# Eight wide matmuls in a row and eight narrow ones in a row, instead of the two in turn: the feature blocks of a hybrid decoder layer

## The chip, the cores and the metric

The kernel runs on one core of a Trainium2 chip. The metric is device time in microseconds (us), the median over three runs. Everything on the core runs as a program of five engines with a queue each: TensorE (PE in the rows; PEld is its weight load), VectorE (DVE), ScalarE (ACT), GpSimd (POOL) and SyncE (SP), which issues the DMAs.

## What is computed

One decoder layer on 256 tokens of 2048 features: an input projection, two mixers side by side (a gated linear recurrence and a sparse attention that keeps 64 of up to 256 keys), a gated merge, an output projection with a layer norm, and a gated ConvFFN with a second layer norm. Cut to what matters here:

```python
h = einsum('btd,de->bte', x, w_in)                  # 2048 -> 12368 features
xr, gr, q, k, v, qi, ki, wi, g_rnn, g_att = split(h)
y_rnn = rg_lru(causal_dwconv(xr)) * gelu(gr)
y_att = dsa_attention(rope(q), rope(k), v, rope(qi), rope(ki), wi, topk)
merged = sigmoid(g_rnn) * y_rnn + sigmoid(g_att) * y_att
x = layer_norm(ALPHA * x + merged @ w_out)
u = causal_dwconv(einsum('btd,df->btf', x, w_up))    # 2048 -> 11264
gate, up = split(u)
x = layer_norm(ALPHA * x + (silu(gate) * up) @ w_down)
```

All of it is in float32. The kernel makes each product from two halves of every operand: `hi`, the number rounded to the type that TensorE multiplies fast (float32r), and `lo`, what is left. A product is hi*hi + hi*lo + lo*hi.

## The kernel before

**Two kinds of product.** A *feature block* (`feature_block`, L161) makes 128 output features on the partitions with the 256 tokens as columns. The moving operand is `xt` (later `x1t`, the same buffer): for each of the 16 slices `k` of the 2048 input features, 512 columns, of which the first 256 are the tokens' hi and the others their lo. The stationary operand is a 128x128 piece of the weights. Per slice there are two matmuls into one PSUM bank of 512 columns: `high()` (L169, its matmul at L170) multiplies all 512 columns by the weight's hi, so that columns 0 to 255 collect hi*hi and 256 to 511 the cross term; `low()` (L173, L174) multiplies the 256 hi columns by the weight's lo and adds to columns 256 to 511. A block is 16 such pairs, high before low, but for the last slice, where the low comes first so that the high closes the bank. There are 181 feature blocks: 1 (80 features wide) and 8 of the indexer, 4 of the keys, 32 of the attention (`q`, `ga`), 48 of the recurrence (`xr`, `gr`, `gn`) and 88 of the ConvFFN (`gate`, `up`).

A *token tile* (`token_tile`, `token_half`, L190 to L202) has tokens on the partitions and 512 features as columns. Here the weights are the moving operand, and all its matmuls are 512 columns wide (L197, L199, L201). Values (`psv`), output projection (`pso`) and `w_down` (`psd`) are made so, and the change doesn't touch them.

**Weights.** A list `order` names the weight tiles (128 x 2048 float32, 1 MB) in the order of use. `load_to` (L102) issues their DMAs on SyncE's queue up to four tiles ahead, into three buffers `raw`. `split_half` (L112) makes hi with ScalarE (L116) and lo with VectorE (L119), for one half of a tile (eight slices) at a time; hi and lo have four buffers of half a tile each, so two tiles. `weights` (L136) asks for the split of the tile after the one that is used next. So a half of hi or lo comes free when the last matmul that reads it is done.

**Around a block.** `project` (L185) makes a block and hands it to a function that evacuates it (`evacuate`, L311: ScalarE copies columns 256 to 511, VectorE adds columns 0 to 255), then `tick` (L146) runs work that was put off by `after` for a number of blocks: the indexer's products (`pl`), the top-k on VectorE (L400, L401), the attention's scores (`ps_s`, L452 to L456, 256 columns each), transposes (`pt`) and gathers (`po`, L487 to L489, 512 columns each), and the recurrence's gates (`pg`, L555 to L557, six matmuls of 256 columns). These stand in TensorE's queue between two blocks. The order of each engine's queue comes from a scheduler that keeps to the program's dependencies and its priorities; it is fixed when the program is built.

Of the kernel before, what the change touches and what calls it, by code (L numbers as in the profile page):

```python
# [16 lines left out]
T = 256  # L17
D = 2048
KT = D // P
# [7 lines left out]
LRU_C = 8.0  # L27
# [7 lines left out]

# Column starts in w_in.
C_XR, C_GR, C_Q, C_K, C_V, C_QI, C_KI, C_GRNN, C_GATT = (
    0, 2048, 4096, 6144, 6656, 7168, 8192, 8272, 10320)

# Columns of the per-feature parameters.  # L40
O_CW, O_CB, O_BA, O_BI, O_LAM, O_G1, O_B1, O_FW, O_FB = (
    0, 64, 80, 96, 112, 128, 144, 160, 424)
N_PAR = 512
# Columns of the constants.
O_ID, O_CI, O_SI, O_PEN = 0, 128, 384, 640
# [4 lines left out]
def hybrid_layer(ctx, tc, x, xT, w_blk, w_ki, w_v, lru_w, par, w_o, w_u, w_d, lnrows, consts, rot, out):  # L50
    nc = tc.nc
# [5 lines left out]

    # ---------------------------------------------------------------- weights
    order = []
# [34 lines left out]
    done = {"load": 0, "split": 0}  # L94
# [42 lines left out]

    # Work that is to wait until some more weight tiles have gone through the tensor engine.
    later = []
# [19 lines left out]

    # Features on partitions, tokens free: columns 0..255 hi*hi, 256..511 the cross terms.  # L160
    def feature_block(key, src, m=P):  # L161
        halves = weights(key)
        ps = psum.tile([P, 512], F32, tag="b", name="psb", bufs=4)
        for k in range(KT):
            hi, lo = halves[k // 8]
            o = (k % 8) * m
            first, last = k == 0, k == KT - 1

            def high():  # L169
                nc.tensor.matmul(ps[:m, :], hi[:, o:o + m], src[:, k, :], start=first, stop=last,  # L170
                                 skip_group_check=True)

            def low():  # L173
                nc.tensor.matmul(ps[:m, T:], lo[:, o:o + m], src[:, k, :T], start=False, stop=False,  # L174
                                 skip_group_check=True)
            if last:
                low()
                high()
            else:
                high()  # L180
                low()
        return ps

    # A block, its evacuation and then whatever waited for it.
    def project(key, fn, src=None, m=P):  # L185
        fn(feature_block(key, xt if src is None else src, m))
        tick()

    # Tokens on partitions, 512 features free; src_hi/src_lo hold features on partitions.
    def token_half(halves, t, ps, k0, hi_at, lo_at, kn):  # L190
# [19 lines left out]

    # The last tiles of a product: the first 128 tokens go through all of them, then the others.
    def token_tiles_held(keys, pss, k0, src, pool, between):
# [13 lines left out]
    nsp = base.tile([P, KT], F32, name="nsp")  # L226
# [6 lines left out]

    # Layer norm of the 128 rows r, 512 columns after another; done(c) takes them.
    def norm(r, g, b, t, done):
# [28 lines left out]

    # ---------------------------------------------------------------- phase 1
    wide = pool("wide")
# [13 lines left out]
    for k0, k1 in zip(cuts, cuts[1:]):  # L280
        r = xraw[k0 // 8][:, k0 % 8 * T:(k0 % 8 + k1 - k0) * T]
        nc.sync.dma_start(r, xT[:, k0 * T:k1 * T])
        s = {0: 0, 4: 1}.get(k0)
        if s is not None:
            nc.sync.dma_start(ki_raw[:, s * kiw:(s + 1) * kiw], w_ki[:, s * kiw:(s + 1) * kiw])
        r = r.rearrange("p (k t) -> p k t", t=T)
        nc.scalar.copy(xt[:, k0:k1, :T], r)
        nc.vector.tensor_sub(xt[:, k0:k1, T:], r, xt[:, k0:k1, :T].bitcast(F32))
        if s is not None:
            splits[0].append(split_half(0, s, ki_raw, kiw))  # L290
    raw = new_raw("raw1")
    halves = [[wst.tile([P, 1024], F32R, tag=tag, name=f"{tag}1_{s}", bufs=4) for tag in ("hi", "lo")]
              for s in range(2)]
    for s in range(4):
        r = raw[:, s * 512:(s + 1) * 512]
        nc.sync.dma_start(r, order[1][1][:, s * 512:(s + 1) * 512])
        hi, lo = (h[:, s % 2 * 512:(s % 2 + 1) * 512] for h in halves[s // 2])
# [21 lines left out]

    # ---- indexer  # L320
    # Scores and attention weights keep queries 128..255 against all keys in columns 0..255,
    # queries 0..127 against keys 0..127 in columns 256..383.
    W2 = T + P
# [86 lines left out]

    # ---- keys and values
    # The parts of a key block lie side by side: keys 0..127 high, low, keys 128..255 high, low.
    kx = pa.tile([P, KV, 2, 2, P], F32R, name="kx")
# [23 lines left out]

    # ---- attention, one group of query heads after another
    def got_q(ps, n, g, pth, ptl):
# [66 lines left out]

    # ---- RG-LRU, four blocks of features at a time
    phm = ExitStack()
# [5 lines left out]

    # nsp = -LRU_C * softplus(-lambda), log1p by its series in e / (2 + e).
    lam = parm[:, O_LAM:O_LAM + KT]
    tiny = lambda name: work.tile([P, KT], F32, tag=name, name=name)
    e, z, z2, acc, neg = (tiny(s) for s in ("l_e", "l_z", "l_z2", "l_acc", "l_neg"))
# [45 lines left out]
    def recur(j0, v):  # L564
        xc, rg, ig, aa, th = (v[s] for s in ("xc", "rg", "ig", "aa", "th"))
        for i in range(NB):
            nc.scalar.activation(th[:, i], rg[:, i], AF.Tanh, scale=nsp[:, j0 + i:j0 + i + 1])
        for i in range(NB):
            nc.scalar.activation(aa[:, i], rg[:, i], AF.Exp, scale=nsp[:, j0 + i:j0 + i + 1])
        # 1 - a^2 = -tanh(log a) * (1 + a^2)  # L570
        nc.scalar.activation(rg, aa, AF.Square)
        nc.vector.scalar_tensor_tensor(th, rg, 1.0, th, op0=ALU.add, op1=ALU.mult)
        nc.scalar.activation(th, th, AF.Sqrt, scale=-1.0)
        nc.vector.tensor_mul(ig, ig, xc)
        nc.vector.tensor_mul(ig, ig, th)
        for i in range(NB):
            nc.vector.tensor_tensor_scan(rg[:, i], aa[:, i], ig[:, i], 0.0, op0=ALU.mult, op1=ALU.add)
# [30 lines left out]

    # ---------------------------------------------------------------- w_out and the first norm
    pho = ExitStack()  # L610
# [46 lines left out]

    # ---------------------------------------------------------------- ConvFFN
    phf = ExitStack()
# [27 lines left out]

    # ---------------------------------------------------------------- w_down and the second norm
    phd = ExitStack()
# [29 lines left out]
def _constants():  # L719
    def angles(rd):  # L720
        half = rd // 2
        inv = np.power(THETA, -np.arange(half, dtype=np.float64) * 2.0 / rd).astype(np.float32)
        ang = np.arange(T, dtype=np.float32)[:, None] * inv[None, :]
        return np.cos(ang.astype(np.float64)).T, np.sin(ang.astype(np.float64)).T

    c = np.zeros((P, N_CONST), np.float32)
    c[:, O_ID:O_ID + P] = np.eye(P)
    cos, sin = angles(16)
    c[:, O_CI:O_CI + T] = 1.0
    for r in (0, 64):  # L730
        c[r:r + 8, O_CI:O_CI + T] = cos
        c[r + 8:r + 16, O_CI:O_CI + T] = cos
        c[r:r + 8, O_SI:O_SI + T] = -sin
        c[r + 8:r + 16, O_SI:O_SI + T] = sin
    cos, sin = angles(32)
    rot = np.zeros((32, 2 * T), np.float32)
    rot[:16, :T], rot[16:, :T] = cos, cos
    rot[:16, T:], rot[16:, T:] = -sin, sin
    # Queries 128..255 against all keys, then queries 0..127 against keys 0..127.
    q = np.arange(P)[:, None]  # L740
    c[:, O_PEN:O_PEN + T] = np.where(np.arange(T)[None, :] > q + P, CAUSAL_FILL, 0.0)
    c[:, O_PEN + T:O_PEN + T + P] = np.where(np.arange(P)[None, :] > q, CAUSAL_FILL, 0.0)
    return c, rot
# [62 lines left out]
```

## Time and profile before

| | us |
|---|---|
| median of 3 runs | 1472.03 |
| lowest, highest | 1469.31, 1472.29 |
| profiled execution: span (nothing stands around it) | 1469.3 |
| TensorE busy | 1430.9 (97%) |
| VectorE busy | 1008.9 (69%) |
| ScalarE busy | 760.5 (52%) |
| GpSimd busy | 269.3 (18%) |

| stage | us from the span's start |
|---|---|
| first block (`ki`) | 5 to 15 |
| indexer and keys (13 blocks with the first) | 5 to 96 |
| values (token tiles) | 96 to 124 |
| attention (32 blocks) | 124 to 328 |
| recurrence (48 blocks) | 328 to 615 |
| output projection, first norm | 615 to 718 |
| ConvFFN (88 blocks) | 718 to 1218 |
| `w_down`, second norm | 1218 to 1469 |

How to read it: a matmul's recorded duration reaches over the start of the next one, since they are pipelined, so busy time of TensorE is no measure of its speed. What tells is the distance from one start to the next. In the timeline, rows that follow each other with the same text are merged (x2), and then the row has the first one's start.

### The profile page before, as it was taken

What the parts mean: (1) busy time and instruction counts of PE and PEld (TensorE: products, weight loads), DVE (VectorE), ACT (ScalarE), POOL (GpSimd) and SP (SyncE); (2) the same over time, 40 slices, a digit from 0 to 9 for tenths busy, and PEclk for the clock granted to TensorE, in tenths of its full rate; (3) what the DMA queues carried; (4) which work ended last, traced back from release to release, by engine and by line L of the source; (5) the groups of instructions that cost most, each with busy time, mean ns of one, the idle gap of its engine ahead of it and who ended that gap; (6) DMA issues with size and microseconds to landing.
All of it is one profiled execution on the core that took longest, in us unless ns stands there. A gap on an engine that the chain in (4) does not pass through costs nothing.

```text
span 1469.3 us, 19909 instructions
## 1 busy us (share of the span) xinstructions
PE 1430.9 (97%) x7718; PEld 1222.6 (83%) x7718; DVE 1008.9 (69%) x1462; ACT 760.5 (52%) x1068; POOL 269.3 (18%) x227
## 2 busy tenths in 40 slices
PE   7989999999999999999799999999999999999996
PEld 6868888888888888888688888888888888888885
DVE  5787766777777777665776777677767775545456
ACT  4444555568777777644344444444444444433342
POOL 3541122220020211110422112211221120000002
PEclk9999999999999999999899999999999999999998
DMA  7435544545545454576355555555555557555552
GB/s 270 161 135 192 180 142 168 186 164 194 203 155 215 143 201 152 192 300 215 143 190 183 183 190 190 183 182 191 189 185 182 191 188 272 206 207 198 190 199 86
DMA packets 42205, 275.41 MB, mean 187 GB/s; under 512 B 4576, under 2 KB 4832, under 8 KB 10240
## 3 DMA queue, kind: packets, MB, share of 16 engines
q1 hardware_dynamic: 42112, 274.16, 52.2%
q8 instruction: 60, 0.98, 0.3%
q14 instruction: 33, 0.27, 0.1%
HBM read 269.94 MB, written 4.19 MB: 187 GB/s over the span
## 4 chain that ended last, share of the span: by engine, by line
PE 91%; DVE 4%; POOL 2%; DMA 1%; issue 1%; ACT 0%; SPq 0%; ACTq 0%; POOLq 0%; DVEq 0%
PE psb L170 44%; PE psb L174 22%; PE psd L201 5%; PE psd L197 5%; PE psd L199 5%; PE pso L201 2%; PE pso L199 2%; PE pso L197 2%; DVE lo L119 1%; DMA cst<-in_consts 1%; POOL qf L333 0%; POOL sh L332 0%; DMA xraw<-in_xT 0%; DVE rg L247 0%; PE psv L199 0%
## 5 line engine op out<-in xcount | busy, mean ns | idle before, releaser
L170 PE MATMUL psb<-xt,hi 128*128 128x512 f32 (+1 forms) x2896 | 1022.7, 400 | 6.4 <-ACT hi L116 5.4
L119 DVE TENSOR_TENSOR lo<-raw,hi 128x1024 fp32r<-128x1024 f32 (+2 forms) x488 | 609.9, 1253 | 361.7 <-ACT hi L116 352.1
L174 PE MATMUL psb<-xt,lo 128*128 128x256 f32 (+1 forms) x2896 | 786.1, 282 | 1.5 <-DVE lo L119 1.3
L116 ACT CAST hi<-raw 128x1024 fp32r<-128x1024 f32 (+1 forms) x488 | 509.5, 1048 | 365.8 <-PE psd L201 126.9
L170 PEld LDWEIGHTS psb<-xt,hi 128*128 128x128 f32 (+1 forms) x2896 | 536.8, 188 | 125.2 <-ACT hi L116 5.4
L174 PEld LDWEIGHTS psb<-xt,lo 128*128 128x128 f32 (+1 forms) x2896 | 547.9, 189 | 18.8 <-DVE lo L119 3.5
L683 POOL TENSOR_TENSOR y<-y 128x256 f32<-128x256 f32 x44 | 68.1, 1549 | 383.8 <-DVE y L675 362.3
L197 PE MATMUL psd<-hi,fh 128*128 128x512 f32 x352 | 136.9, 389 | 0.0
L199 PE MATMUL psd<-lo,fh 128*128 128x512 f32 x352 | 136.9, 389 | 0.0
L201 PE MATMUL psd<-hi,fl 128*128 128x512 f32 x352 | 136.9, 389 | 0.0
L675 DVE SCALAR_TENSOR_TENSOR y<-u,parm,y 128x255 f32<-128x255 f32 (+1 forms) x176 | 85.1, 484 | 6.2
L199 PEld LDWEIGHTS psd<-lo,fh 128*128 128x128 f32 x352 | 66.1, 188 | 13.8
L201 PEld LDWEIGHTS psd<-hi,fl 128*128 128x128 f32 x352 | 66.1, 188 | 13.7
L197 PEld LDWEIGHTS psd<-hi,fh 128*128 128x128 f32 x352 | 66.1, 188 | 13.5
L313 ACT COPY ev<-psb 128x256 f32<-128x256 f32 (+1 forms) x181 | 65.6, 362 | 0.8 <-PE psb L170 0.8
L684 ACT CAST fh<-y 128x256 fp32r<-128x256 f32 x44 | 17.9, 407 | 90.8 <-POOL y L683 90.8
L238 POOL TENSOR_SCALAR rstd<-mv 128x1 f32<-128x1 f32 x4 | 3.1, 778 | 294.8 <-DVE mv L236 294.8
L199 PE MATMUL pso<-lo,mh 128*128 128x512 f32 x128 | 49.9, 390 | 0.0
L197 PE MATMUL pso<-hi,mh 128*128 128x512 f32 x128 | 49.9, 390 | 0.0
L201 PE MATMUL pso<-hi,ml 128*128 128x512 f32 x128 | 49.8, 389 | 0.0
L331 POOL TENSOR_TENSOR qf<-qf,rots 32x256 f32<-32x256 f32 x16 | 15.5, 971 | 151.6 <-DVE sh L330 151.6
L681 ACT ACTIVATE y<-y 128x256 f32<-128x256 f32 x44 | 18.4, 419 | 47.0 <-DVE y L675 47.0
(172 smaller groups left out, 1028.0 us busy)
## 6 DMA issues: line engine op xcount, KB each, us to landing
raw<-in_w_blk SPq DMA_DIRECT2D x91, 1024.0 KB, 4.8
raw<-in_w_u SPq DMA_DIRECT2D x88, 1024.0 KB, 4.7
raw<-in_w_d SPq DMA_DIRECT2D x44, 1024.0 KB, 4.7
raw<-in_w_o SPq DMA_DIRECT2D x16, 1024.0 KB, 4.8
raw<-in_w_v SPq DMA_DIRECT2D x4, 1024.0 KB, 4.8
lwr<-in_lru_w SPq DMA_DIRECT2D x4, 512.0 KB, 3.7
g<-in_lnrows SPq DMA_DIRECT2D x2, 1024.0 KB, 6.6
xres<-in_x SPq DMA_DIRECT2D x4, 512.0 KB, 7.3
```

The costliest lines, as they stand in the source:

```text
L116: nc.scalar.copy(hi[:, :w], raw[:, s * w:(s + 1) * w])
L119: eng.tensor_sub(lo[:, o:o + step], raw[:, s * w + o:s * w + o + step], hi[:, o:o + step].bitcast(F32))
L170: nc.tensor.matmul(ps[:m, :], hi[:, o:o + m], src[:, k, :], start=first, stop=last, skip_group_check=True)
L174: nc.tensor.matmul(ps[:m, T:], lo[:, o:o + m], src[:, k, :T], start=False, stop=False, skip_group_check=True)
L197: nc.tensor.matmul(ps, hi_at(k, t), hi[:, o:o + 512], start=first, stop=False, skip_group_check=True)
L199: nc.tensor.matmul(ps, hi_at(k, t), lo[:, o:o + 512], start=False, stop=False, skip_group_check=True)
L201: nc.tensor.matmul(ps, lo_at(k, t), hi[:, o:o + 512], start=False, stop=last, skip_group_check=True)
L313: nc.scalar.copy(t[:m], ps[:m, T:])
L675: nc.vector.scalar_tensor_tensor(y[:, s:], u[:, :T - s], w(tap), y[:, s:], op0=ALU.mult, op1=ALU.add)
L681: nc.scalar.activation(yg, yg, AF.Silu)
L683: nc.gpsimd.tensor_mul(yg, yg, yu)
L684: nc.scalar.copy(fh[:, j], yg)
```

## The change

The 32 matmuls of a feature block stay as they are, with the same operands, and come in another order: for the first half of the slices eight highs and then eight lows; for the second half seven highs, eight lows and the last high. The rest of the difference is in comments alone, so line numbers move: the high's matmul is L166 in the changed kernel, the low's L171.

```diff
     def feature_block(key, src, m=P):
         halves = weights(key)
         ps = psum.tile([P, 512], F32, tag="b", name="psb", bufs=4)
-        for k in range(KT):
-            hi, lo = halves[k // 8]
-            o = (k % 8) * m
-            first, last = k == 0, k == KT - 1
-
-            def high():
-                nc.tensor.matmul(ps[:m, :], hi[:, o:o + m], src[:, k, :], start=first, stop=last,
-                                 skip_group_check=True)
-
-            def low():
-                nc.tensor.matmul(ps[:m, T:], lo[:, o:o + m], src[:, k, :T], start=False, stop=False,
-                                 skip_group_check=True)
-            if last:
-                low()
-                high()
-            else:
-                high()
-                low()
+        def high(k):
+            hi, o = halves[k // 8][0], k % 8 * m
+            nc.tensor.matmul(ps[:m, :], hi[:, o:o + m], src[:, k, :], start=k == 0, stop=k == KT - 1,
+                             skip_group_check=True)
+
+        def low(k):
+            lo, o = halves[k // 8][1], k % 8 * m
+            nc.tensor.matmul(ps[:m, T:], lo[:, o:o + m], src[:, k, :T], start=False, stop=False,
+                             skip_group_check=True)
+
+
+        for s in range(2):
+            ks = range(8 * s, 8 * s + 8)
+            for k in ks[:8 - s]:
+                high(k)
+            for k in ks:
+                low(k)
+        high(KT - 1)
         return ps
```

On TensorE, the border of the last two ConvFFN blocks before (`hi_1` and `lo_1` are the second halves of a tile's weights, `hi_0` and `lo_0` the first of the next; 512 or 256 is the number of columns):

```order
L174 MATMUL psb<-xt,lo_1_11175 128x256
L170 MATMUL psb<-xt,hi_1_11174 128x512
L174 MATMUL psb<-xt,lo_1_11175 128x256 x2
L170 MATMUL psb<-xt,hi_1_11174 128x512
L170 MATMUL psb<-xt,hi_0_11224 128x512
L174 MATMUL psb<-xt,lo_0_11225 128x256
L170 MATMUL psb<-xt,hi_0_11224 128x512
```

The same two blocks in the changed kernel, down to the first token tile of `w_down`:

```order
L166 MATMUL psb<-xt,hi_0_11170 128x512 x8
L171 MATMUL psb<-xt,lo_0_11171 128x256 x8
L166 MATMUL psb<-xt,hi_1_11174 128x512 x7
L171 MATMUL psb<-xt,lo_1_11175 128x256 x8
L166 MATMUL psb<-xt,hi_1_11174 128x512
L166 MATMUL psb<-xt,hi_0_11224 128x512 x8
L171 MATMUL psb<-xt,lo_0_11225 128x256 x8
L166 MATMUL psb<-xt,hi_1_11228 128x512 x7
L171 MATMUL psb<-xt,lo_1_11229 128x256 x8
L166 MATMUL psb<-xt,hi_1_11228 128x512
L197 MATMUL psd<-hi_0_11276,fh 128x512
```

Each high left its low; the last high of a block and the first eight of the next are now nine in a row.

On VectorE, between the keys' last blocks and the value product (`score` is the top-k's table, `lo_0` a half of the first value tile's weights, `kx` the keys):

```order
 L389 SCALAR_TENSOR_TENSOR score<-rl,wi,score 128x128
 L400 MAX m_990<-score 128x8
-L400 MAX m_993<-score 128x8
-L401 MATCH_REPLACE score<-m_990,score 128x256
-L401 MATCH_REPLACE score<-m_993,score 128x128
 L119 TENSOR_TENSOR lo_0_997<-raw_788,hi_0_996 128x1024
 L421 TENSOR_TENSOR kx<-kf,kx 128x2x128
+L401 MATCH_REPLACE score<-m_990,score 128x256
+L400 MAX m_993<-score 128x8
 L400 MAX m_1050<-score 128x8
+L401 MATCH_REPLACE score<-m_993,score 128x128
```

The split of the value weights and the keys' lo moved ahead of three small operations of the top-k. ScalarE's queue has a few such neighbours that changed places; those of GpSimd and SyncE are the same as before.

## Rows read from the trace of the kernel before

**Rows 1.** The page: busy us (share) xinstructions; the chain by line

```profile
PE 1430.9 (97%) x7718; PEld 1222.6 (83%) x7718; DVE 1008.9 (69%) x1462; ACT 760.5 (52%) x1068; POOL 269.3 (18%) x227
...
PE psb L170 44%; PE psb L174 22%; PE psd L201 5%; PE psd L197 5%; PE psd L199 5%; PE pso L201 2%; PE pso L199 2%; PE pso L197 2%; DVE lo L119 1%; DMA cst<-in_consts 1%; POOL qf L333 0%; POOL sh L332 0%; DMA xraw<-in_xT 0%; DVE rg L247 0%; PE psv L199 0%
```

**Rows 2.** Stages: start:end, length, busy us (x) by engine, PEclk, DMA, GB/s

```profile
84.00:126.00 42.00, 38.14 (x178) 30.39 (x175) 35.72 (x88) 18.80 (x28) 11.10 (x12) 0.96 0.50 175
720.00:1218.00 498.00, 498.00 (x2814) 431.95 (x2814) 355.79 (x524) 240.12 (x350) 100.09 (x86) 1.00 0.52 183
```

**Rows 3.** Timeline of TensorE, ConvFFN: start us, us, engine line op tiles xcount

```profile
850.24 0.63 PE L170 MATMUL psb<-xt,hi 128*128 128x512 f32 x2
850.71 0.28 PE L174 MATMUL psb<-xt,lo 128*128 128x256 f32 x1
850.83 0.40 PE L170 MATMUL psb<-xt,hi 128*128 128x512 f32 x1
...
851.89 0.40 PE L170 MATMUL psb<-xt,hi 128*128 128x512 f32 x1
```

**Rows 4.** Timeline of TensorE, last feature block and first token tile

```profile
1217.71 0.40 PE L170 MATMUL psb<-xt,hi 128*128 128x512 f32 x1
1217.95 0.40 PE L197 MATMUL psd<-hi,fh 128*128 128x512 f32 x1
1218.18 0.39 PE L199 MATMUL psd<-lo,fh 128*128 128x512 f32 x1
...
1218.63 0.39 PE L197 MATMUL psd<-hi,fh 128*128 128x512 f32 x1
```

**Rows 5.** Timeline of TensorE, an LRU block right behind a gate product

```profile
508.96 0.40 PE L170 MATMUL psb<-xt,hi 128*128 128x512 f32 x1
...
514.29 0.62 PE L170 MATMUL psb<-xt,hi 128*128 128x512 f32 x2
```

**Rows 6.** Timeline of TensorE, deep in the token tiles of w_down

```profile
1300.23 0.39 PE L197 MATMUL psd<-hi,fh 128*128 128x512 f32 x1
```

**Rows 7.** Timeline of TensorE, gather product of attention

```profile
229.67 0.39 PE L487 MATMUL po<-pth,vh 128*128 128x512 f32 x1
...
231.76 0.39 PE L170 MATMUL psb<-xt,hi 128*128 128x512 f32 x1
```

**Rows 8.** Timeline of TensorE, an attention block and the scores behind it

```profile
199.01 0.39 PE L170 MATMUL psb<-xt,hi 128*128 128x512 f32 x1
...
204.66 0.28 PE L452 MATMUL ps_s<-kx,qh 128*128 128x256 f32 x1
...
205.25 0.49 PE L475 MATMUL pt<-ident,pr 128*128 128x128 f32 x3
```

**Rows 9.** Timeline of TensorE, LRU stage: start, a wait before gates, end

```profile
333.67 0.63 PE L170 MATMUL psb<-xt,hi 128*128 128x512 f32 x2
...
415.23 0.39 PE L170 MATMUL psb<-xt,hi 128*128 128x512 f32 x1
...
417.91 0.39 PE L170 MATMUL psb<-xt,hi 128*128 128x512 f32 x1
...
614.93 0.40 PE L197 MATMUL pso<-hi,mh 128*128 128x512 f32 x1
```

**Rows 10.** Waits of TensorE: us in total, times, longest

```profile
PE psv L199 <- DVE lo L119: 3.5, 3, 2.0
```

**Rows 11.** Timeline of TensorE, first block, with idle before and releaser

```profile
9.63 0.71 PE L170 MATMUL psb<-xt,hi 128*80 128x512 f32 x1 [0.98 <-DVE xt L288]
10.15 0.41 PE L174 MATMUL psb<-xt,lo 128*80 128x256 f32 x1
10.36 0.63 PE L170 MATMUL psb<-xt,hi 128*80 128x512 f32 x1
```

**Rows 12.** Timeline of TensorE, value product

```profile
112.06 0.40 PE L197 MATMUL psv<-hi,xt 128*128 128x512 f32 x1
...
114.36 0.39 PE L199 MATMUL psv<-lo,xt 128*128 128x512 f32 x1
```

## The prediction

> **What bounds the kernel now.** The page's busy table and chain come first: TensorE is busy nearly all the span, and two lines of the feature blocks, the 512-column matmul (below: a high) and the 256-column one (a low), hold 66% of the chain that ended last [rows 1]. So a nanosecond on the spacing of these matmuls counts, unless something else is late in that stage. The table by stage says where that is: in the ConvFFN stage (720 to 1218 us) TensorE is busy all 498 us, VectorE 356, ScalarE 240, all at the full granted clock of 1.00 (2.4 GHz); in the stage of keys and values (84 to 126 us) it is busy 38 of 42, so something else is late there [rows 2]. Of a matmul I read only when it starts and when the next one starts: the durations overlap.
>
> The timeline inside a ConvFFN block shows the spacing. From the high at 850.83 to the one three pairs later at 851.89 are 1.06 us, 0.353 per high and low [rows 3]. From the last two highs that stand together at 850.24 [rows 3] to the last high of the stage at 1217.71 [rows 4] are 367.47 us and 65 blocks: **5.653 us a block**, and no waits. But the same 32 matmuls can cost less: a block of the LRU stage right behind a gate product starts at 508.96, its last high and the next block's first start together at 514.29, and with 0.23 for the first of these two it took 514.52 - 508.96 = **5.56 us** [rows 5]. Same tiles, same shapes, same order; only what ran just before differs. So the alternation has a cheap rhythm and a dear one, and about 0.09 us a block lies between them.
>
> **What the change does.** All 181 feature blocks keep their 32 matmuls and weight loads. The order now has eight highs, eight lows, seven highs, eight lows, one high, and with the next block's eight the last high makes a run of nine. Nothing is added or taken from any other engine, and the order of SyncE's and GpSimd's queues is the same. On VectorE and ScalarE a few instructions change places with a neighbour.
>
> *Price of a high in a run.* The nearest rows are the token tiles: 512 columns, one new stationary tile each, one PSUM bank. From 1218.63 [rows 4] to 1300.23 [rows 6] they make 360 steps in 81.60 us: 0.2267 each. How fast a feature block's high falls to that is seen where the last block meets the first token tile: 1217.71, 1217.95, 1218.18, then 0.2267 on [rows 4]. The first two steps take 0.47, that is 0.016 over two at 0.2267. The other end is the gather product, nine in a row from 229.67 to 231.76, 0.232 each [rows 7]. I take 0.2267: it has hundreds of rows, and the entry is the feature block's own.
>
> *Price of a low in a run.* The scores are five 256-column matmuls in a row, 204.66 to 205.25: 0.118 each [rows 8]; pairs of lows in a block take 0.12. I take 0.119.
>
> *A block after.* Eight highs: 8 x 0.2267 + 0.016 = 1.830. Eight lows: 8 x 0.119 = 0.952. Twice the sum is **5.56 us**, which is also what the cheap blocks take now, by other rows.
>
> *The sum, by stage.* ConvFFN: 88 x (5.653 - 5.56) = 8.2 us. LRU: from 333.91 (0.24 behind the row at 333.67) to 614.93, 281.0 us for 47 blocks, 16 gate products of six lows (6 x 0.118 = 0.71 each) and three waits in front of gates; one wait is 417.91 - 415.23 - 0.23 - 0.71 = 1.74 [rows 9]. (281.0 - 11.4 - 5.2) / 47 = 5.626 a block: some are cheap already. 48 x 0.066 = 3.2 us. The three waits hang on a chain of ScalarE, GpSimd and VectorE that starts at the previous group's last block, so the three blocks that TensorE does meanwhile become 3 x 3 x 0.07 = 0.6 us of longer waiting: 2.6 net. Attention: the block from 199.01 to 204.66 took 5.65 [rows 8], and I count 31 of 32 such: 31 x 0.09 = 2.8 us.
>
> The first 13 blocks, of the indexer and the keys, I put at nothing: 13 x 0.09 = 1.2 us gained is covered, since the value product behind them waits 3.5 us for VectorE's weight splits already [rows 10] and would wait that much longer. VectorE puts two of its splits a little earlier there, ahead of two or three small top-k operations, which I count as up to 1 us, either way. The very first block loses: its highs wait for x (the one at 9.63 waited 0.98 us), and its lows now fill no such hole: four lows of 10.36 - 10.15 = 0.21 come behind it, 0.9 us [rows 11]. That too is ahead of the value product's waits, so it shortens them. Both ends of this stage, -1 and +1 us, stay in the range.
>
> What else could come out: the highs read their weight half first and are done with it after 1.83 us instead of 2.8, so ScalarE may overwrite it earlier, and the lows need VectorE's half later than before. No new wait follows from either; the halves are split a block ahead. VectorE's 356 us for 88 blocks are 4.0 a block [rows 2], far from 5.56.
>
> Sum: 8.2 + 2.6 + 2.8 = **13.6 us** off. The profiled execution has 1469.3 us, the shortest of the three times, so it becomes 1455.7. The median lies 2.7 above it, at 1472.03; I expect the same distance: **1458.5 us**.
>
> **Rivals.**
> *The highs of a run keep the gather's spacing.* 0.232 gives a block of 2 x (8 x 0.232 + 0.952) = 5.62: 88 x 0.03 + 32 x 0.03 + nothing in LRU = 4 us off, 1468. For it: feature blocks have the same kind of moving operand, an activation. Against it: the entry in [rows 4].
>
> *Order is nothing.* If a step's time belonged to its columns and its weight load alone, the same 32 would take the same time, 1472. Against it are the two prices of the same block [rows 3, 5]. The Trainium skill, "TensorE: Matmul & The Clock Gate", section "Back-to-back issue gap", has such a rule: columns over 2.4 GHz plus 2.5 ns, an estimate of 325 ns for a high and a low in any order. By that rule the sum would be nil. The trace disagrees with its size, 353 and 347 ns, and with its being one number.
>
> *Slower.* What stands in a feature block now when two highs meet is dear: two steps take 0.47 (850.24 to 850.71), the first 0.24 of it [rows 3, 4]. If a run of highs with xt as moving operand stays at 0.235 to 0.24 a step, as every change of stationary tile behind a matmul of this kind would then cost, a block takes 5.66 to 5.74. In the middle, 5.70, this is 88 x 0.05 + 48 x 0.07 + 32 x 0.05 = 9 us, so 1481. It decides from 0.233 a high on, where a block is back at 5.63. Against it: the second step is 0.23 already, and the third 0.2267, when the next rows are token tiles. A settling that takes many steps is in the trace once, in the value product, whose stage has a mean granted clock of 0.96 [rows 2]: 112.06 to 114.36, ten steps of 0.23 [rows 12]. Runs of eight would never be through with that; this is the gather's case again in price.
>
> That the change doesn't do what it says I exclude by the order of the built program.
>
> **How the numbers follow.** Forecast 0.64; gather's price 0.12; order is nothing 0.10; slower 0.14. About 0.2% (3 us) is what a measurement of this kernel tells from no change: faster 0.64 + 0.08 = 0.72, same 0.04 + 0.10 = 0.14, slower 0.14. The range starts at 1453 (a cheaper entry into the runs, the first stage's gain not covered, a median nearer its lowest) and reaches to 1472.5, over the gather's case and most of no change; it leaves out the slower case and the tails.
>
> **What would show it.** In the timeline of a ConvFFN block: highs 0.227 apart from the third of a run on, lows 0.12, blocks 5.56 apart, and all blocks alike. The ConvFFN stage shorter by 8 us, the LRU stage by 2.6, attention by 2.8, up to 126 us nothing; the value product's wait longer, or its start a little earlier. Highs at 0.232 or more in the middle of a run make the forecast wrong, and so does any new wait of a feature block for a weight split.

## The result, and the profile after

The changed kernel takes **1463.37 us** (median of 4 runs, 1462.41 to 1464.15) against 1471.72 of the kernel before, run beside it: ratio 0.9946, 95% interval 0.9932 to 0.996. It is faster by 8.4 us, some 0.5%. The forecast was 1458.5, so the direction held and the gain was 5 us smaller than the 13.6 of the sum.

The profiled execution has a span of 1460.4 us and a time of 1462.41, so some 2 us do stand around a span, where the text ahead took nothing. The span of 1469.3 before therefore belongs to an execution of about 1471.3, and not to the shortest one of 1469.31. Spans are compared below: 1469.3 to 1460.4, 8.9 less. First the page (columns as in [rows 1]): the same two lines head the chain, and TensorE is as full as it was.

```profile
PE 1421.3 (97%) x7718; PEld 1225.0 (84%) x7718; DVE 996.4 (68%) x1462; ACT 754.4 (52%) x1068; POOL 250.6 (17%) x227
...
PE psb L166 40%; PE psb L171 20%; PE psd L199 5%; PE psd L201 5%; PE psd L197 5%; PE pso L201 2%; PE pso L199 2%; PE pso L197 2%; DVE lo L119 1%; POOL sh L332 1%; POOL qf L333 1%; ACT hi L116 1%; POOL qf L331 1%; POOL gn L603 1%; DMA cst<-in_consts 1%
```

The spacing is read from TensorE's timeline in the ConvFFN stage of the changed kernel, as in [rows 3]. Each row is one run now, with its first start.

```profile
862.42 2.23 PE L166 MATMUL psb<-xt,hi 128*128 128x512 f32 x9
864.49 1.12 PE L171 MATMUL psb<-xt,lo 128*128 128x256 f32 x8
865.44 1.78 PE L166 MATMUL psb<-xt,hi 128*128 128x512 f32 x7
867.05 1.11 PE L171 MATMUL psb<-xt,lo 128*128 128x256 f32 x8
868.01 2.23 PE L166 MATMUL psb<-xt,hi 128*128 128x512 f32 x9
...
873.59 2.23 PE L166 MATMUL psb<-xt,hi 128*128 128x512 f32 x9
```

A block is 873.59 - 868.01 = 5.58, over the stage **5.587 us**, and all blocks but the first are alike. Nine highs take 864.49 - 862.42 = 2.07, 0.03 more than nine at 0.2267; seven take 1.61, 0.02 more. Eight lows take 0.95 to 0.96. Start by start, a run goes 0.234, 0.235, 0.229, 0.232, 0.231, and from the sixth step 0.227: 0.027 on entry, where I had 0.016. The first low behind a run takes 0.113, the second 0.119, the others 0.120, so 0.020 is left of each entry. TensorE's timeline where the last block meets the first token tiles (compare [rows 4]) shows the same settling with other operands:

```profile
1208.79 0.40 PE L166 MATMUL psb<-xt,hi 128*128 128x512 f32 x1
1209.03 0.40 PE L197 MATMUL psd<-hi,fh 128*128 128x512 f32 x1
...
1209.72 0.39 PE L197 MATMUL psd<-hi,fh 128*128 128x512 f32 x1
...
1210.41 0.39 PE L197 MATMUL psd<-hi,fh 128*128 128x512 f32 x1
```

Seven steps take 1.62, 0.03 over the settled 7 x 0.2267. In the kernel before, with the same token tiles behind two lows instead of eight, it was through after two steps [rows 4]. So what ran before changes the settling, with the same operands.

The stages by the starts of their first matmuls, before to after; one profiled execution stands for each kernel:

| stage | before | after | change | forecast |
|---|---|---|---|---|
| up to the start of attention | 124.33 | 124.83 | +0.5 | 0 (-1 to +1) |
| attention: blocks | 181.5 | 180.2 | -1.3 | -2.8 |
| attention: between blocks | 19.9 | 21.3 | +1.4 | 0 |
| recurrence: its blocks | | | -1.7 | -3.2 |
| recurrence: three waits before gates | | | -2.0 | +0.6 |
| output projection, norm | 103.60 | 103.62 | 0 | 0 |
| ConvFFN, 88 blocks | 499.4 | 493.6 | -5.8 | -8.2 |
| `w_down`, norm | 251.4 | 251.4 | 0 | 0 |

**Attention has a new wait.** From the waits of TensorE in the changed kernel (us in total, times, longest):

```profile
PE pg L556 <- DVE xl L547: 1.9, 3, 0.6
...
PE pt L475 <- DVE pr L469: 1.5, 1, 1.5
```

The second is new: a transpose waits for the scaled softmax numerators `pr`. TensorE's timeline has the place, the last of five scores and the first transpose; before, these two stood 0.12 apart (160.81 and 160.93):

```profile
161.10 0.27 PE L456 MATMUL ps_s<-kx,ql 128*128 128x256 f32 x1
162.86 0.52 PE L475 MATMUL pt<-ident,pr 128*128 128x128 f32 x3 [1.49 <-DVE pr L469]
```

VectorE's timeline of the kernel before, and then of the changed one, says why. `sm` (L463) is the scaled row maximum that ScalarE's Exp needs; `ql` (L446) waits for GpSimd's rotation and ScalarE's `qh`:

```profile
155.40 0.37 DVE L463 TENSOR_SCALAR sm<-sm 128x2 f32<-128x2 f32 x1
...
158.76 0.43 DVE L446 TENSOR_TENSOR ql<-qf,qh 128x256 fp32r<-128x256 f32 x1 [1.87 <-ACT qh L445]
```

```profile
160.28 0.42 DVE L446 TENSOR_TENSOR ql<-qf,qh 128x256 fp32r<-128x256 f32 x1 [2.56 <-ACT qh L445]
160.62 0.16 DVE L463 TENSOR_SCALAR sm<-sm 128x2 f32<-128x2 f32 x1
```

The scheduler gave the changed program another order on VectorE's queue: `sm` is now behind `ql`, though it needs nothing from it, and sits out ql's wait of 2.56 us. Between the two blocks, 0.84 us became 2.69.

**The recurrence's waits shrank.** TensorE's timeline at the gates that waited in [rows 9], first gate matmul of the kernel before:

```profile
416.19 0.38 PE L555 MATMUL pg<-xh,lwh 128*128 128x256 f32 x1 [0.57 <-ACT xh L546]
```

The same place in the changed kernel:

```profile
415.31 0.39 PE L166 MATMUL psb<-xt,hi 128*128 128x512 f32 x1
415.62 0.38 PE L555 MATMUL pg<-xh,lwh 128*128 128x256 f32 x1
416.65 0.38 PE L556 MATMUL pg<-xl,lwh 128*128 128x256 f32 x1 [0.65 <-DVE xl L547]
...
417.34 1.99 PE L166 MATMUL psb<-xt,hi 128*128 128x512 f32 x8
```

From the block's last high to the next block are 2.03 us, 2.68 before [rows 9]; the wait for `xl` stayed, the one for `xh` went. ScalarE's timeline, where this chain begins (kernel before, then changed), shows the reason: its cast of a weight half into `hi` waits for the last matmul that reads the buffer, and what stands behind it in the queue waits along:

```profile
401.40 1.05 ACT L116 CAST hi<-raw 128x1024 fp32r<-128x1024 f32 x1 [1.38 <-PE psb L170]
...
403.76 1.06 ACT L600 ACTIVATE gn<-gn 128x1024 f32<-128x1024 f32 x1
```

```profile
400.81 1.05 ACT L116 CAST hi<-raw 128x1024 fp32r<-128x1024 f32 x1 [0.52 <-PE psb L166]
...
403.18 1.06 ACT L600 ACTIVATE gn<-gn 128x1024 f32<-128x1024 f32 x1
```

With the highs of a half done first, the buffer is free earlier, the cast waits 0.52 in place of 1.38, and the sigmoid of `gn` starts 0.58 earlier, while the last high before the gates stands where it stood (415.23 and 415.31). From this sigmoid to the cast that makes `xh` are 11.97 us before and 11.98 after. The chain between them runs through the queues: GpSimd's work on `gn`, ScalarE's `mh` behind it and then its next weight casts, VectorE's weight split, and behind that the last step of `xc`.

### The profile page after: what moved, and what is told of

Its sections match the earlier page's. It is cut to its first block, busy times and chain, and to the rows that moved or that the text cites. A ratio compares the mean times of both kernels' runs of the same rounds, so it can differ in the third digit from the quotient of the medians.

```text
span 1460.4 us, 19897 instructions
## 1 busy us (share of the span) xinstructions
PE 1421.3 (97%) x7718; PEld 1225.0 (84%) x7718; DVE 996.4 (68%) x1462; ACT 754.4 (52%) x1068; POOL 250.6 (17%) x227
## 4 chain that ended last, share of the span: by engine, by line
PE 85%; POOL 5%; DVE 5%; ACT 2%; issue 1%; DMA 1%; SPq 0%; ACTq 0%; DVEq 0%; POOLq 0%
PE psb L166 40%; PE psb L171 20%; PE psd L199 5%; PE psd L201 5%; PE psd L197 5%; PE pso L201 2%; PE pso L199 2%; PE pso L197 2%; DVE lo L119 1%; POOL sh L332 1%; POOL qf L333 1%; ACT hi L116 1%; POOL qf L331 1%; POOL gn L603 1%; DMA cst<-in_consts 1%
## 5 line engine op out<-in xcount | busy, mean ns | idle before, releaser
L166 PE MATMUL psb<-xt,hi 128*128 128x512 f32 (+1 forms) x2896 | 741.1, 395 | 7.5 <-ACT hi L116 5.5
L166 PEld LDWEIGHTS psb<-xt,hi 128*128 128x128 f32 (+1 forms) x2896 | 522.0, 189 | 102.2 <-ACT hi L116 5.5
L171 PEld LDWEIGHTS psb<-xt,lo 128*128 128x128 f32 (+1 forms) x2896 | 396.1, 191 | 29.0 <-issue 0.4
L171 PE MATMUL psb<-xt,lo 128*128 128x256 f32 (+1 forms) x2896 | 404.8, 283 | 0.0
L683 POOL TENSOR_TENSOR y<-y 128x256 f32<-128x256 f32 x44 | 32.5, 738 | 402.8 <-DVE y L675 402.8
L201 PEld LDWEIGHTS psd<-hi,fl 128*128 128x128 f32 x352 | 66.1, 188 | 13.6
L331 POOL TENSOR_TENSOR qf<-qf,rots 32x256 f32<-32x256 f32 x16 | 26.4, 1653 | 146.9 <-DVE sh L330 129.2
```

What stands on the lines that cost most here:

```text
L201: nc.tensor.matmul(ps, lo_at(k, t), hi[:, o:o + 512], start=False, stop=last, skip_group_check=True)
L331: nc.gpsimd.tensor_mul(v, v, cos)
L683: nc.gpsimd.tensor_mul(yg, yg, yu)
```

## Experiments

The theory after this: (a) the price of a block depends on the length of the runs, through a cost at each entry into a run of highs; (b) an earlier release of `hi` shortens waits that hang on ScalarE's queue; (c) the new wait of attention comes from VectorE's order. Rivals: (a') alternating as such is what was dear, and any longer run is as good as another; (b') the gates' waits changed because queues were reordered, not through the release; (c') the wait comes from the matmuls' new timing. All diffs are against the changed kernel where nothing else is said.

### Pure alternation

Before, the alternation broke at the end of each block, where two lows and two highs met. Here it doesn't.

```diff
-            nc.tensor.matmul(ps[:m, T:], lo[:, o:o + m], src[:, k, :T], start=False, stop=False,
+            nc.tensor.matmul(ps[:m, T:], lo[:, o:o + m], src[:, k, :T], start=False, stop=k == KT - 1,
...
-        for s in range(2):
-            ks = range(8 * s, 8 * s + 8)
-            for k in ks[:8 - s]:
-                high(k)
-            for k in ks:
-                low(k)
-        high(KT - 1)
+        for k in range(KT):
+            high(k)
+            low(k)
```

> Every block alternates from first to last (high, low, ..., high 15, low 15): no two lows and no two highs meet any more at a block's border. Theory A: that border is what throws the alternation into its dear rhythm, block after block; without it the ConvFFN stage stays in the cheap one, 3 pairs in 1.04 us, 5.55 us a block instead of 5.653 of the kernel before and 5.587 of the changed one: ConvFFN 9 us shorter than before, the whole between 1457 and 1463, by how much of attention and recurrence stays cheap. Rival B: the dear rhythm is the alternation's own, and a gate product breaks it for a block: 5.65 a block, 1472 as before. Beside it: a weight half of hi comes free as late as in the kernel before, so by the theory that the earlier release shortened the three waits before gates in the recurrence, these are 1.7 us again; if they were shortened by instructions that changed places, they may stay at 1.0.

Measured: 1469.77 us, ratio 0.9981 (0.996 to 1.0001), and the ten runs fall apart: three at 1461.1 to 1462.5, one at 1465.5, six at 1469.6 to 1471.7. The profiled one is of the long kind. TensorE's timeline in ConvFFN, two highs with 18 pairs between them:

```profile
849.83 0.40 PE L166 MATMUL psb<-xt,hi 128*128 128x512 f32 x1
...
856.18 0.40 PE L166 MATMUL psb<-xt,hi 128*128 128x512 f32 x1
```

6.35 / 18 = 0.353 a pair, as in the kernel before. At the three gates of the recurrence, from the block's last high to the next block are 1.31, 2.66 and 2.67 us: two are as long as before. The same kernel was profiled once more, to see a run of the short kind.

> The pure alternation once more, for another profile: four of its ten executions were 1461 to 1465.5 us and the others 1469.6 to 1471.7, and the profiled one, 1469.97, was all in the dear rhythm. Theory: the rhythm is a state that an execution falls into and keeps, so a shorter execution has ConvFFN blocks of 5.55 us, 88 x 0.1 = 9 us less. Rival: the shorter ones save their time elsewhere, and every profile has 5.65.

Measured: 1463.43 us. The same stretch of its timeline:

```profile
849.86 0.39 PE L166 MATMUL psb<-xt,hi 128*128 128x512 f32 x1
...
856.10 0.39 PE L166 MATMUL psb<-xt,hi 128*128 128x512 f32 x1
```

6.24 / 18 = 0.347 a pair. All distances between ConvFFN blocks but the first are 5.546 or 5.547 here, against 5.649 to 5.661 in the other profile, and the stage takes 490.06 us against 498.4. In attention and the recurrence the blocks take the same in both profiles (181.6 and 181.5, 275.2 and 275.2). So the same program falls into one rhythm or the other at the start of this stage, and keeps it for 490 us. Rival (a') is half right: alternating is dear only in one of two rhythms. What chooses between them stays open.

The rhythm also goes into what follows. The first token tiles of `w_down` come behind a single low in both profiles. In the dear one their first step takes 0.236, and the next already 0.226. In the cheap one nine steps pass before 0.227 is reached, the tenth start being the second line of TensorE's timeline here:

```profile
1210.05 0.39 PE L193 MATMUL psd<-hi,fh 128*128 128x512 f32 x1
...
1212.13 0.39 PE L193 MATMUL psd<-hi,fh 128*128 128x512 f32 x1
```

They go 0.230, 0.234, 0.236, 0.224, 0.231, 0.235, 0.229, 0.232, 0.231. So the number of lows ahead doesn't fix the settling either.

### Runs of 16, of 4 and of 2

```diff
-        for s in range(2):
-            ks = range(8 * s, 8 * s + 8)
-            for k in ks[:8 - s]:
-                high(k)
-            for k in ks:
-                low(k)
+        for k in range(KT - 1):
+            high(k)
+        for k in range(KT):
+            low(k)
         high(KT - 1)
```

> Fifteen highs, sixteen lows, the last high: one run of 16 highs and one of 16 lows a block. Theory: a run of highs behind a run of lows pays about 27 ns on its first five steps and a run of lows gets 8 back, once a run, and the rest goes at 226.7 and 120 ns. So a block of one entry takes 16 x 0.2267 + 16 x 0.120 + 0.02 = 5.567 us against 5.587 of the changed kernel: 168 x 0.02 = 3.4 us less, about 1460. Rival: highs with this moving operand have a mean of 0.231 whatever the length of the run: 5.587 a block, 1463.4.

Measured: **1454.27 us** (1453.11 to 1455.47), ratio 0.9892 (0.9877 to 0.9907). TensorE's timeline in ConvFFN:

```profile
849.78 3.82 PE L166 MATMUL psb<-xt,hi 128*128 128x512 f32 x16
853.44 2.08 PE L171 MATMUL psb<-xt,lo 128*128 128x256 f32 x16
855.35 3.82 PE L166 MATMUL psb<-xt,hi 128*128 128x512 f32 x16
```

Sixteen highs take 3.66, again 0.03 over 16 x 0.2267, now once a block: 5.567, as expected. ConvFFN went from 493.6 to 490.7. That is a third of the 9.1 us to the changed kernel; attention's wait of 1.85 is not there, since VectorE's order differs here, and the gates' waits are gone (between blocks of the recurrence 11.8 us in place of 14.4), where ScalarE's and VectorE's order differs as well.

```diff
-        for s in range(2):
-            ks = range(8 * s, 8 * s + 8)
-            for k in ks[:8 - s]:
-                high(k)
+        for s in range(0, KT, 4):
+            ks = range(s, s + 4)
+            for k in ks:
+                if k < KT - 1:
+                    high(k)
             for k in ks:
                 low(k)
         high(KT - 1)
```

> Runs of four highs and four lows. Theory (a run of highs behind lows pays its first five steps): 233.5 + 235.5 + 228.5 + 232.5 for four highs, 113 + 119 + 120 + 120 for four lows with the steps 227 at their borders counted in, about +15 ns a run over 4 x (226.7 + 120): 5.547 + 4 x 0.015 = 5.61 us a block in the ConvFFN, between the changed kernel's 5.587 and the 5.653 of the alternation; about 1466. Rival (a fixed mean of 231 and 119 in any run): 5.60; rival (runs shorter than the settling fall back into the dear rhythm): 5.65.

Measured: 1475.84 us (1474.77 to 1478.09), ratio 1.003 (1.002 to 1.004), the one order that is slower than before. Undisturbed blocks are 5.595 and 5.612 in turn. But from 917 us on, two blocks of every six in ConvFFN take 6.05 and 6.31. In TensorE's timeline such a block stretches in its middle:

```profile
1001.07 0.63 PE L171 MATMUL psb<-xt,lo 128*128 128x256 f32 x4
1001.84 1.19 PE L166 MATMUL psb<-xt,hi 128*128 128x512 f32 x4
1003.10 0.74 PE L171 MATMUL psb<-xt,lo 128*128 128x256 f32 x4
```

Four lows take 0.77 where 0.47 is usual, four highs 1.26 in place of 0.93. ScalarE's timeline at that place:

```profile
1000.43 0.41 ACT L685 CAST fh<-y 128x256 fp32r<-128x256 f32 x1 [3.79 <-POOL y L684]
1000.75 1.04 ACT L116 CAST hi<-raw 128x1024 fp32r<-128x1024 f32 x1
```

The weight cast stands behind an `fh` that waited 3.79 us, and comes to TensorE just too late: the high at 1001.84 starts when the cast of 1000.75 is done. This is read from the trace; putting the casts ahead was not tried. The price of an undisturbed block came out near the estimate. By this reading, the order of ScalarE's queue took more than the runs gave.

The same edit with 2 in place of 4:

> Runs of two. Theory as for four: 233.5 + 235.5 + 113 + 119 would be 701 ns for two pairs, 5.61 us a block; but the settling was read behind runs of eight lows, so the first step may be as dear as 240: up to 5.65. If the price of a run's entry is what makes the alternation dear, the block price falls in the order 1, 2, 4, 8, 16 of the run's length; if two is as cheap as sixteen, the entry is not what is paid.

Measured: 1464.85 us (1463.15 to 1464.94), ratio 0.995 (0.9935 to 0.9965); every block of ConvFFN but the first 5.600, the stage 493.9, no late ones. By length of run a ConvFFN block takes:

| run | 1 | 2 | 4 | 8 | 16 |
|---|---|---|---|---|---|
| us a block | 5.653 or 5.547 | 5.600 | 5.595 to 5.612 | 5.587 | 5.567 |

Against settled steps, 16 x (0.2267 + 0.120) = 5.547, the excess is 0.020 for one entry a block at 16 and 0.040 for two at 8. That is one price, 0.020 an entry, and step by step the entry is the same behind eight lows and behind sixteen. Runs of 4 and 2 end before they have settled, and pay less at each of more entries: 0.048 to 0.065 for four, 0.053 for eight. Alternating pays 0.106 in its dear rhythm and nothing in its cheap one.

### The release of hi

First, hi's first half held longer: its last high behind its lows.

```diff
-        for s in range(2):
-            ks = range(8 * s, 8 * s + 8)
-            for k in ks[:8 - s]:
-                high(k)
-            for k in ks:
-                low(k)
+        for k in range(7):
+            high(k)
+        for k in range(8):
+            low(k)
+        for k in range(7, KT - 1):
+            high(k)
+        for k in range(8, KT):
+            low(k)
         high(KT - 1)
```

> Seven highs, eight lows, then high 7 and highs 8 to 14, eight lows, the last high: runs of eight as in the changed kernel, but the first half of hi is read until behind the first lows, so ScalarE may overwrite it about 0.95 us later. Theory: the earlier release is what shortened the three waits in front of the recurrence's gates (1.7 us before, 1.0 or so in the changed kernel), since ScalarE's queue stands behind the cast that waits for it. Then the waits are 1.7 us again and the recurrence 2 us longer, 1465.5, at an unchanged 5.587 a block in the ConvFFN. Rival: the waits shortened for another reason (instructions that changed places in other queues): they stay, 1463.4.

Measured: 1463.16 us (1461.67 to 1465.22), ratio 0.9953 (0.9937 to 0.997); blocks 5.587. Two of three gates wait for `xh` again, the first of these in TensorE's timeline:

```profile
486.57 0.39 PE L557 MATMUL pg<-xh,lwh 128*128 128x256 f32 x1 [0.98 <-ACT xh L548]
487.60 0.38 PE L558 MATMUL pg<-xl,lwh 128*128 128x256 f32 x1 [0.65 <-DVE xl L549]
```

The third waits for `xl` alone. But this run changed the order of other queues as well (attention's new wait is gone here too), and at these gates that is what counts: the sigmoid of `gn` starts no later before the block's last high (12.31 us, against 12.13 in the changed kernel), and from it to `xh` are 13.2 us in place of 12.0. The alternating kernel has the same other order there, and 13.2 us too. So a changed order can bring the wait by itself, as (b') says, and this run doesn't speak for (b).

The runs of 4 and of 2 do. At the first of the three gates they have the same order from the cast to `xh` as both kernels, on ScalarE, VectorE and GpSimd. In the runs of 2, the cast on ScalarE and then the gate on TensorE:

```profile
400.19 1.05 ACT L116 CAST hi<-raw 128x1024 fp32r<-128x1024 f32 x1 [1.25 <-PE psb L166]
...
415.01 0.38 PE L556 MATMUL pg<-xh,lwh 128*128 128x256 f32 x1 [0.63 <-ACT xh L547]
```

| | before | runs of 2 | runs of 4 | changed (8) |
|---|---|---|---|---|
| the cast waits for `hi` | 1.38 | 1.25 | 0.99 | 0.52 |
| from the sigmoid to `xh` | 11.97 | 12.00 | 12.01 | 11.98 |
| the gate waits for `xh` | 0.57 | 0.63 | 0.38 | none |

With the order fixed, the chain keeps its length, and the gate's wait goes away with an earlier release. The other test leaves the matmuls of the kernel *before* as they are and gives `hi` a fifth half-tile buffer:

```diff
-        hi = at.tile([P, 1024], F32R, tag="hi", name=f"hi{i}_{s}", bufs=bufs)
+        hi = at.tile([P, 1024], F32R, tag="hi", name=f"hi{i}_{s}", bufs=bufs if i in spare else 5)
...
-    halves = [[wst.tile([P, 1024], F32R, tag=tag, name=f"{tag}1_{s}", bufs=4) for tag in ("hi", "lo")]
+    halves = [[wst.tile([P, 1024], F32R, tag=tag, name=f"{tag}1_{s}", bufs={"hi": 5, "lo": 4}[tag])
+               for tag in ("hi", "lo")]
```

> The kernel before, with five buffers of half a tile for hi instead of four, so that ScalarE's cast of the next half finds a free buffer earlier, with the alternation as it was. Theory (the release of hi is what held ScalarE's queue, and the three waits before the recurrence's gates behind it): the waits of 1.7 us shrink by 0.7 us or more each, the blocks keep 5.653 us, the kernel gains 2 to 5 us, 1465 to 1468. Rival (the order of instructions in the queues decides): they stay, 1470.

Measured: **1461.93 us** (1460.38 to 1462.73), ratio 0.9935 (0.9918 to 0.9951), with the ConvFFN blocks, from the fourth on, still at the dear 5.65. ScalarE's timeline, the place that was at 401.40 before:

```profile
394.30 1.05 ACT L116 CAST hi<-raw 128x1024 fp32r<-128x1024 f32 x1
...
396.67 1.06 ACT L601 ACTIVATE gn<-gn 128x1024 f32<-128x1024 f32 x1
```

The cast no longer waits, and the sigmoid starts 13.9 us before the block's last high in place of 11.5. All three gates are free of waits, for `xl` too; the recurrence is 5.1 us shorter, and attention starts at 119.60 in place of 124.33.

Not all of this is the release. VectorE's timeline has another order at the gates, first the kernel before and then this one:

```profile
415.62 1.21 DVE L119 TENSOR_TENSOR lo<-raw,hi 128x1024 fp32r<-128x1024 f32 x1
416.76 0.41 DVE L547 TENSOR_TENSOR xl<-xc,xh 128x256 fp32r<-128x256 f32 x1
```

```profile
409.26 0.42 DVE L548 TENSOR_TENSOR xl<-xc,xh 128x256 fp32r<-128x256 f32 x1 [0.47 <-ACT xh L547]
409.60 1.22 DVE L119 TENSOR_TENSOR lo<-raw,hi 128x1024 fp32r<-128x1024 f32 x1
```

The wait of 0.65 for `xl` went because `xl` no longer stands behind a weight split. That is (b') at work. So (b) is shown for the waits for `xh`, and (b') holds for those for `xl`. The earlier start of attention is clear: 119.1 to 120.0 in the three programs with five buffers, 123.1 to 126.2 in the nine profiles with four, two of the same program being 2.2 apart. How much of it is the release and how much the order, no run here separates. One buffer gives as much as the whole change, with TensorE's order left as it was.

### The scale of the row maximum first

```diff
-        nc.vector.tensor_scalar(sm[:, 0:2], sm[:, 0:2], -SCALE, None, op0=ALU.mult)
+        with tc.high_priority(PRIO):
+            nc.vector.tensor_scalar(sm[:, 0:2], sm[:, 0:2], -SCALE, None, op0=ALU.mult)
```

> The changed kernel, with a higher priority for the one small VectorE operation of the softmax that scales the row maxima, so that it stands ahead of the split of ql as in the kernel before. Theory: the new wait of 1.85 us in attention (a transpose that waits for the normalized weights) comes from that one place in VectorE's order, because the exponentials behind it start 1 us later: the gap of 2.69 us becomes 0.84 again and the kernel takes 1461.5. Rival: TensorE just comes earlier and would wait anyway: the gap stays over 2 us, 1463.4.

Measured: 1461.41 us (1459.6 to 1462.47), ratio 0.9939 (0.9924 to 0.9954). Between the two blocks are 1.07 us in place of 2.69, with the block order unchanged, and the median is 2.0 lower. The intervals of the two kernels overlap, and the profiled execution is no shorter (1460.5 against 1460.4, with 1.3 more up to attention and 1.1 more in the output projection), so the time alone would not prove it; the gap does. (c) holds against (c').

### Both together

Runs of 16 with five `hi` buffers, and the changed kernel with five; both edits as above.

> Runs of 16 together with five buffers for hi. If the runs' length and the buffer act on different things, they add where they don't share a wait: blocks as in the runs of 16 (5.567), the waits before the gates stay gone, and the value product's stage is shorter by the 4.7 us that the fifth buffer gave the kernel before: 1454.3 - 4.7 = 1449.6 us. If the fifth buffer's 4.7 us were a release that the longer run of highs gives anyway, 1454.

> The changed kernel with five buffers for hi. Theory (the changed kernel's gain in the recurrence was an earlier release of hi): blocks stay at 5.587; the value stage gives 4.7, what is left of the waits before the gates 2.6: 1463.4 - 7.3 = 1456.1 us. If the buffer helped the kernel before only by what the new order gives already, 1463 (at most 4.7 less, 1458.7).

Measured: **1447.51 us** (1446.38 to 1448.03), ratio 0.9844 (0.9828 to 0.9861), and **1451.57 us** (1450.91 to 1451.97), ratio 0.987 (0.9856 to 0.9885). Both beat both kernels, and both came in below what was expected. In the changed kernel the fifth buffer took 4.8 us off the start of attention (120.02 against 124.83), 3.0 off between the recurrence's blocks, and attention's new wait as well, since VectorE's order is that of the kernel before again: 1.85, which I had not counted. At the gates with eight in a row and five buffers, TensorE's timeline has 0.94 us from the last high to the next block, where 2.03 stood:

```profile
408.61 0.39 PE L166 MATMUL psb<-xt,hi 128*128 128x512 f32 x1
...
409.55 2.01 PE L166 MATMUL psb<-xt,hi 128*128 128x512 f32 x8
```

With the waits now alike in both, most of the 4.1 us between these two kernels is the second entry of each block: 168 blocks behind the first stage x 0.020 (5.587 - 5.567) = 3.4. The two profiled executions are 5.5 apart; the rest lies up to the start of attention (1.0), in ConvFFN's first block (1.0) and in the output projection (0.2).

## Why the prediction was right and wrong

**Right:** what bounds the kernel, that a run of highs falls from 0.235 to 0.227 and a low is 0.12, that all ConvFFN blocks become alike, and that the first stage gives nothing that can be told. The gather's price is out as the price of a whole run (a block would be 5.62), and the slower case is out as a price (5.66 to 5.74).

**Wrong, the entry.** The step "the first two steps take 0.47, that is 0.016 over two at 0.2267" took the entry from behind two lows [rows 4] and set it behind eight. There it takes five steps and 0.027. Two entries and the rounding of 5.564 make a block 0.027 dearer than my 5.56, over 88 blocks 2.4 us of the 5 that were missed, and over the recurrence's 48 most of the 1.5 missed there. "A settling that takes many steps is in the trace once", I wrote of the value product [rows 12], and put it with a rival; the forecast itself should have carried part of it.

**Wrong, the count in attention.** "I count 31 of 32 such" rested on one block [rows 8]. The blocks went from 181.5 to 180.2, 0.04 each on the mean. 25 of the 32 gave 0.05 to 0.08. The other seven lost up to 0.04: six of them, all behind transposes, took 5.645 to 5.655 before and 5.68 after, and one behind a gather took 5.561 before. With the price, this is 1.5 us of the miss.

**Wrong, "No new wait follows from either".** It was argued from the weight halves alone. Whoever moves when 5792 matmuls release their operands also moves what a scheduler sees, and it swapped `sm` and `ql`: 1.85 us lost, or 2.0 by the time. I had listed that neighbours change places and priced those before the value product, but not those in attention.

**Wrong in sign, the gates.** "The three blocks that TensorE does meanwhile become 3 x 3 x 0.07 = 0.6 us of longer waiting" missed that the chain's own start hangs on the release of `hi`, which I named a paragraph later as harmless. It came out 2.0 us shorter. That one error was in the change's favour, and hides part of the others: entries 2.4, attention's blocks 1.5, its wait and the other gaps 1.4, the recurrence's blocks 1.5 and the first stage 0.5 make 7.3 too little, less 2.6 for the gates gives 4.7, the difference of 13.6 and 8.9. That the total came out as near as it did is in part luck.

**A pairing that did no harm.** The sum took the profiled execution for the shortest and added 2.7 us to come to the median. It was one of about 1471.3, near the median; but the median less 13.6 is the forecast within 0.1 us either way.

**Order is nothing** is refuted three times: by 5.587 against 5.653, by the table of run lengths, and by one program in two rhythms. The Trainium skill, "TensorE: Matmul & The Clock Gate", section "Back-to-back issue gap", gives columns over 2.4 GHz plus 2.5 ns, with no term for what ran before, and calls it the gap of an isolated matmul: by that formula an estimate of 16 x 325 ns = 5.20 us a block. No order here came below 5.546, and the runs show 0.2267 and 0.120 for a settled step in place of its 0.216 and 0.109.

## What to carry to other kernels

When matmuls of two widths alternate, read the spacing start to start, and look for the same mix at two prices in one trace; if there are two, group the widths in long runs, and price the entry from more than one place: here it took one step, two, five or nine, by what ran before. Before pricing an order on TensorE, look at what its buffers' release holds up: an engine that waits for a free buffer at the head of its queue delays all behind it, and one buffer more may be worth the whole reordering. In a program whose queues a scheduler orders, compare the small operations of every stage, since one of 0.16 us behind a wait of 2.6 took a fifth of this gain.

## What the runs showed of the hardware

- Strict alternation of 512 and 256 columns has two rhythms, 0.347 and 0.353 us a pair, at a granted clock of 1.00; one program shows either, and keeps it over a stage of 490 us or more. In the ConvFFN stage they differ by 8.3 us. That they make the ten runs fall into two groups is likely, with one profile of each kind.
- A run of 512-column matmuls behind eight or sixteen of 256 starts at 0.234 and needs five steps to 0.227; behind two of 256 it needs two, and behind one it needs one or nine, by the rhythm that ran before. What keeps this memory, no run here shows.
